# Block 0's expert outputs: rows of v gathered by token and summed over slots in four column groups of TensorE, in place of rows gathered by slot and summed token by token

## The chip, the cores and the metric

One core of one Trainium2 chip. The metric is the device time of one execution in microseconds (us). The kernel before was run three times.

## What is computed

One decoder layer over 512 tokens of width 1024: a mixer (matrix memory and differential attention), cross attention into 256 memory rows, and PEER, a channel mixer that picks 128 of 16384 experts for each token; then a final norm. Everything is float32. The change touches PEER alone, and of it the last line, for the first 128 tokens:

```python
def peer(h, w_pq, sub_keys, peer_u, peer_v):        # 4 blocks of 128 tokens
    def block(xb):
        q = (xb @ w_pq).reshape(PEER_BLOCK, PEER_HEADS, 2, PEER_HALF)
        sc = jnp.einsum('thcd,hcnd->thcn', q, sub_keys)
        ...                                          # top 16 of each half, top 16 of their sums
        u = peer_u[eidx]                             # eidx: 128 tokens x (8 heads x 16) experts
        act = jax.nn.gelu(jnp.einsum('td,thkd->thk', xb, u), approximate=False)
        coef = (gate * act).astype(xb.dtype)
        return jnp.einsum('thk,thkd->td', coef, peer_v[eidx])
```

With c[t, s] the coefficient of token t's slot s (128 slots), the sum is y[t] = sum over s of c[t, s] * v[eidx[t, s]], with 4 KB for each row of v.

## The kernel before

**Order of the work.** Block 0 (tokens 0 to 127) goes first through mixer, cross attention and key scores, then `route(0)` (top-k on DVE) gives its expert indices `eidx` and gates. Blocks 1 to 3 go together through the mixers (about 300 to 625 us) and then through `tail([2, 3, 1])`: cross attention (`cs`, `ct`, `co`, `cot`), query projection (`pqt`) and key scores (`rs`). Then come the routes of blocks 2 and 3 and of block 1. For blocks 2 and 3 the kernel builds a dense table W of gates over all experts, 64 tiles of 4 tokens each (L1052 to L1077: DVE compares, ACT scales and copies them to `oi` and `oj`, PE multiplies them into `wps`, ACT copies the product to W). From 1019 us to the end, 128 expert blocks are multiplied for blocks 2 and 3 in the dense stage. Blocks 0 and 1 take the sparse way, with gathered rows.

**The feeder.** Block 0's sparse work is woven into the work on blocks 1 to 3. `feed(where)` adds `PACE[where]` steps to what is owed at certain points of the program, and takes as many steps from a generator. The first generator, `sparse_dots(0)`, gathers u rows (one gather of 128 rows, 512 KB, for each slot) and takes dot products. The second, `sparse_sums(0)`, gathers the v rows of slot s for all 128 tokens (partition = token, L904, an indirect DMA that POOL issues into one of four buffers tagged `u`), and adds them:

- in the tail (slots 0 to 67) on DVE: `vacc = v * c + vacc`, L991 and L993;
- from the route stage on (slots 68 to 111) on PE: ACT scales an identity matrix by the slot's coefficients (`dg`, L985), and two matmuls with 128x128 weights `dg` and 128x512 of the rows add into PSUM (`vpe`, L987);
- slots 112 to 127 on DVE again.

A scheduler orders each engine's instructions when the program is built; at run time each engine works through its own list and waits where something is not ready. From the route stage on the gathers are kept in the program's order.

**PSUM.** The tail has three pools of banks (`ps` 3, `pa` 3, `pb` 2), the route and W stages two (`ps` 4, `pa` 4).

Names for what follows: a *slot* is one gather of the kernel before; a *tile* is one of W's 64 tiles; `trp` are the three transposes at the end of `route(2)` and `route(3)`.

Of the kernel before, what the change touches and what calls it, by code (L numbers as in the profile page):

```python
# [20 lines left out]
S = 512  # L21
D = 1024
# [8 lines left out]
SLOTS = HEADS * TOPK  # L31
# [3 lines left out]

U0A, U1A = (1,), ()

PACE = {"proj": 0.9, "ml": .8, "da": 1, "ca": 1.2, "route": 4, "W": .6, "half": 1.05}

LOW = ("pool",) * 8 + ('pool', 'dve', 'dve', 'dve', 'pool', 'dve', 'dve', 'dve')  # L40
LOW_FIRST = ('dve', 'dve', 'dve', 'dve', 'dve', 'dve', 'dve', 'dve')

PE_END = 111


def skewed(items, *stages, after=None):
# [39 lines left out]
def layer_kernel(ctx, tc, x, mem, norm_mix_g, w_in, conv_w, b_igate, b_fgate, ml_norm_g,  # L86
# [16 lines left out]
    keep = ctx.enter_context(tc.tile_pool(name="keep", bufs=1))  # L103
    dram = ctx.enter_context(tc.tile_pool(name="dram", bufs=1, space=DRAM))
    pctx = [ExitStack()]
    ctx.callback(lambda: pctx[0].close())

    def open_psum(name, **n):
        pctx[0].close()
        pool = pctx[0].enter_context(tc.tile_pool(name=name, bufs=1, space=PSUM))  # L110
        return [lambda nm, tag=tag, k=k: pool.tile([P, 512], F32, tag=tag, name=nm, bufs=k) for tag, k in n.items()]

    psums = open_psum("psumf", ps=3, pa=3, pb=2)

# [9 lines left out]
    ident = const.tile([P, P], F32, name="ident")  # L124
# [46 lines left out]
    def ft(shape, tag, name, bufs=2, dt=F32):  # L171
        return home[0].tile(shape, dt, tag=tag, name=name, bufs=bufs)
# [243 lines left out]
    feeder, owed = [], [0.0]  # L416
    in_step, on_pe, in_psum = [False], [False], [None]

    def feed(where, n=1):

        owed[0] += n * PACE[where]
        while owed[0] >= 1 and feeder:
            if next(feeder[0], None) is None:
                feeder.pop(0)
            else:
                owed[0] -= 1
# [16 lines left out]
        proj_tok(w_cv, 0, D, mT, 2, "mv", ev_v)  # L443
        nc.sync.dma_start(mv_d, mv)

    small, convs = [], [None]

    def queued_behind(ins, first):
        if first is not None:
            tc.add_manual_dep(ins.ins, first.ins.name,  # L450
                              mybir.DependencyInfo(mybir.DependencyClass.NoSync, mybir.DependencyReason.DATA))
# [359 lines left out]
    def route(T, scs, dense, tile_):  # L811

        gate = ft([P, SLOTS], "gate", f"gate{T}", bufs=1) if dense else keep.tile([P, SLOTS], F32, tag="gate", name=f"gate{T}", bufs=2)
        eidx = None if dense else keep.tile([P, SLOTS], I32, tag="eidx", name=f"eidx{T}", bufs=2)
        If = ft([P, SLOTS], "If", f"If{T}", bufs=1)
        Jf = ft([P, SLOTS], "Jf", f"Jf{T}", bufs=1)
        for q in range(2):
# [66 lines left out]
            nc.vector.reciprocal(gsum, gsum)  # L884
            nc.vector.tensor_tensor(gt, gt, gsum.unsqueeze(2).to_broadcast([P, 4, TOPK]), op=OP.mult)
            feed("route")
        if not dense:
            return eidx, gate
        tr = ft([P, 3, P], "tr", f"tr{T}")
        tp = ps(f"trp{T}")  # L890
        for i, t in enumerate((If, Jf, gate)):
            nc.tensor.transpose(tp[:, i * P:(i + 1) * P], t, ident)
        nc.scalar.copy(tr, tp[:, :3 * P].rearrange("p (a t) -> p a t", a=3))
        return tr

    def u_tile(name, shape=(P, D), dt=F32):
        return keep.tile(list(shape), dt, tag="u", name=name, bufs=4)


    to_gather, ahead = [], []  # L900

    def gather(src, eidx, s, name):
        u = u_tile(name)
        g = nc.gpsimd.indirect_dma_start(out=u, out_offset=None, in_=src,  # L904
                                         in_offset=bass.IndirectOffsetOnAxis(ap=eidx[:, s:s + 1], axis=0))
        if on_pe[0]:
            tc.keep_in_program_order(g)
# [12 lines left out]
    def finish(blocks, ys):  # L920

# [22 lines left out]
                nc.vector.scalar_tensor_tensor(x2[:, sl], x2[:, sl], r[:, 0:1], gf[:, sl], op0=OP.mult, op1=OP.mult)  # L944
                nc.sync.dma_start(outf[T * P:(T + 1) * P, sl], x2[:, sl])

    coefs, lane = {}, [None]

    def sparse_dots(T, eidx, gate, aside):

# [19 lines left out]
        nc.vector.tensor_mul(gate, act, gate)  # L970
        coefs[T] = gate

    def sparse_sums(T, eidx):

        act = coefs[T]
        acc = in_psum[0](f"vaccp{T}") if in_psum[0] else keep.tile([P, D], F32, tag="hv", name=f"vacc{T}", bufs=2)
        pe, last = None, None
        for s in range(SLOTS):
            v = gathered()
            c = act[:, s:s + 1]  # L980
            if on_pe[0] and 0 < s <= PE_END:
                if pe is None:
                    pe = [pa(f"vpe{T}{n}") for n in range(2)]
                dg = rp.tile([P, P], F32, tag="dg", name=f"dg{T}_{s}", bufs=2)
                nc.scalar.activation(dg, ident, AF.Copy, scale=c)  # L985
                for n in range(2):
                    nc.tensor.matmul(pe[n], lhsT=dg, rhs=v[:, n * 512:(n + 1) * 512],  # L987
                                     start=last is None, stop=s == PE_END)
                last = s
            elif s == 0:  # L990
                nc.vector.tensor_scalar(acc, v, c, None, op0=OP.mult)  # L991
            else:
                nc.vector.scalar_tensor_tensor(acc, v, c, acc, op0=OP.mult, op1=OP.add)  # L993
            if pe and s == PE_END:
                for n in range(2):
                    sl = slice(n * 512, (n + 1) * 512)
                    nc.vector.tensor_add(acc[:, sl], acc[:, sl], pe[n])
                pe = None
            lane[0] = pe
            yield s  # L1000
        finish([T], [acc])

# [14 lines left out]
    plan(0, r0[0])  # L1017
    feeder.append(sparse_dots(0, *r0, aside=U0A))
    feeder.append(sparse_sums(0, r0[0]))
    x1 = mixers(1, 3, hT1)  # L1020
    fctx.close()
    rp = rctx.enter_context(tc.tile_pool(name="routes", bufs=1, side="right", reuse_waits="tile"))
    home[0] = bctx.enter_context(tc.tile_pool(name="tail", bufs=1, reuse_waits="tile"))
    rings.update({"big": 2, "w": 8, "w4": 6})
    scs = {}
# [7 lines left out]
    def score(T, pq):  # L1033
        scs[T] = key_scores(T, pq, wide)

    order = [2, 3, 1]
    tail(order, [x1[T - 1] for T in order], True, w4, score)
    bctx.close()
    home[0] = rp
    psums[:] = open_psum("psumd", ps=4, pa=4)  # L1040
    on_pe[0] = True
    trs = [route(T, scs[T], True, scratch) for T in (2, 3)]
    r1 = route(1, scs[1], False, scratch)
# [6 lines left out]
    iota4 = op.tile([P, P, 4], BF16, name="iota4")  # L1050
    nc.gpsimd.tensor_copy(iota4, iota_n.unsqueeze(2).to_broadcast([P, P, 4]))
    for tt in range(NDENSE):  # L1052
        tr = trs[tt]
        ij = op.tile([P, 2, P], BF16, tag="ij", name=f"ij{tt}", bufs=1)
        nc.vector.tensor_copy(ij, tr[:, 0:2, :])
        for t4 in range(0, P, 4):
            eqs = []
            for a in range(2):
                e = op.tile([P, P, 4], BF16, tag=f"eq{a}", name=f"eq{tt}{t4}{a}", bufs=2)
                nc.vector.tensor_tensor(e, iota4, ij[:, a, t4:t4 + 4].unsqueeze(1).to_broadcast([P, P, 4]), op=OP.is_equal)  # L1060
                eqs.append(e)
            oi = op.tile([P, 4, P], F32, tag="oi", name=f"oi{tt}{t4}", bufs=3)
            oj = op.tile([P, 4, P], F32, tag="oj", name=f"oj{tt}{t4}", bufs=3)
            wps = ps(f"wps{tt}{t4}")
            nc.scalar.copy(oj, eqs[1].rearrange("p j q -> p q j"))
            for q in range(4):
                g = tr[:, 2, t4 + q:t4 + q + 1]
# [13 lines left out]
    owed[0] = 0.0  # L1081
    on_pe[0] = False
    rctx.close()
    pools = pctx[0].enter_context
    pctx[0].close()
    pq_ = pctx[0].enter_context(tc.tile_pool(name="psume", bufs=1, space=PSUM))
    in_psum[0] = lambda nm: pq_.tile([P, D], F32, tag="hv", name=nm, bufs=1)
    dp = ctx.enter_context(tc.tile_pool(name="dense", bufs=1, side="right", reuse_waits="tile"))
# [145 lines left out]
```

## Time and profile before

| what | us |
|---|---|
| runs of the kernel before | 1885.2, 1883.58, 1882.15 (median 1883.58) |
| the profiled execution's own time | 1875.28 |
| its span, first to last instruction | 1873.5 |
| busy: PE / DVE / POOL / ACT | 1591.3 / 1449.2 / 1062.8 / 806.9 |
| mean granted TensorE clock | 0.924 of full speed |

The span is the time from the first instruction to the last in one profiled execution; busy times are what each engine spent in instructions that the profiler recorded. "PEld" is TensorE's loading of weights, which overlaps the products. A float32 matmul leaves two records on PE, so counts of records are twice those of matmuls. A wait is the idle time of an engine before an instruction, with what ended it.

### The profile page before, as it was taken

To read this page: it belongs to the slowest core of one execution; us is meant where nothing else is said; L and a number is where in the kernel's file an instruction comes from. 1 tells how busy PE (TensorE), PEld (TensorE's weight loads), DVE (VectorE), ACT (ScalarE), POOL (GpSimd) and SP (SyncE) were. 2 spreads that over 40 slices of the span, in tenths; PEclk is the share of its full clock that TensorE was granted. 3 is DMA by queue.
4 is the path that set the end of the run, shared out by engine and by line. 5 is a ranking of instruction groups with operands and counts; after the bars stand their busy time and mean duration, and the time that the engine had idled before them with its cause. 6 is when DMAs were issued, how large, how long until landed. Compare 5 with 4: busy or idle time off the path is not lost.

```text
span 1873.5 us, 27679 instructions
## 1 busy us (share of the span) xinstructions
PE 1591.3 (85%) x9223; PEld 1330.1 (71%) x9223; DVE 1449.2 (77%) x3042; ACT 806.9 (43%) x1836; POOL 1062.8 (57%) x864
## 2 busy tenths in 40 slices
PE   7999796787647788899966999999999999999986
PEld 6798686685337467763655877777787778777765
DVE  4354498878878467999985888889888888888874
ACT  3553423535432122133999444444444444444433
POOL 2000136677766456345430877778787777777754
PEclk9899878898569899899988999999999999999998
DMA  7758615787777988677660999999999999999983
GB/s 240 236 185 272 217 50 175 231 294 262 234 237 248 369 289 295 203 217 257 191 229 32 323 339 336 331 331 335 326 339 333 331 330 334 337 333 322 335 303 118
DMA packets 211456, 501.15 MB, mean 267 GB/s; under 512 B 20793, under 2 KB 90481, under 8 KB 210545
## 3 DMA queue, kind: packets, MB, share of 16 engines
q0 software_dynamic: 74304, 270.57, 42.6%
q1 hardware_dynamic: 137008, 228.82, 36.0%
q8 instruction: 72, 1.18, 0.3%
q14 instruction: 72, 0.58, 0.1%
HBM read 490.93 MB, written 8.39 MB: 267 GB/s over the span
## 4 chain that ended last, share of the span: by engine, by line
DMA 26%; DVE 23%; PE 15%; issue 13%; ACT 11%; POOL 10%; SPq 1%; POOLq 0%; ACTq 0%; DVEq 0%
DMA vd<-in_peer_v_dram 13%; DMA v<-in_peer_v_dram,eidx 7%; DMA u<-in_peer_u_dram,eidx 5%; DVE uL L1129 4%; DVE u L966 4%; ACT vH L1137 4%; POOL vL L1138 4%; PE cqt_o L320 3%; POOL u L904 3%; ACT uH L1128 2%; DVE vacc L993 2%; PE vpe L987 2%; ACT oi L1069 2%; DVE ua L1156 1%; DVE vaccp L993 1%
## 5 line engine op out<-in xcount | busy, mean ns | idle before, releaser
L904 POOL DMA_INDIRECT u<-in_peer_u_dram,eidx x256 | 309.5, 1209 | 220.4 <-DVE u L966 104.9
L904 POOL DMA_INDIRECT v<-in_peer_v_dram,eidx x256 | 284.7, 1112 | 242.0 <-DVE vaccp L993 57.8
L1129 DVE TENSOR_TENSOR uL<-ud,uH 128x512 fp32r<-128x512 f32 x256 | 307.6, 1238 | 112.7 <-ACT uH L1128 110.2
L1138 POOL TENSOR_TENSOR vL<-vd,vH 128x512 fp32r<-128x512 f32 x256 | 352.8, 1395 | 57.4 <-ACT vH L1137 34.6
L312 PE MATMUL ua<-hH,uH 128*128 128x256 f32 x1024 | 290.4, 284 | 3.1 <-ACT hH L1101 3.1
L313 PE MATMUL ua<-hL,uH 128*128 128x256 f32 x1024 | 290.8, 284 | 0.2 <-DVE hL L1102 0.2
L314 PE MATMUL ua<-hH,uL 128*128 128x256 f32 x1024 | 290.6, 284 | 0.0
L313 PE MATMUL acc<-vL,pH 128*128 128x512 f32 x512 | 223.2, 436 | 53.6 <-POOL vL L1138 50.9
L1158 ACT CAST pH<-ua 128x256 fp32r<-128x256 f32 x128 | 47.7, 372 | 396.5 <-DVE ua L1156 396.5
L312 PE MATMUL acc<-vH,pH 128*128 128x512 f32 x512 | 203.3, 397 | 9.2 <-ACT vH L1137 9.2
L312 PEld LDWEIGHTS ua<-hH,uH 128*128 128x128 f32 x1024 | 196.8, 192 | 8.7 <-ACT hH L1101 3.3
L314 PE MATMUL acc<-vH,pL 128*128 128x512 f32 x512 | 202.7, 396 | 0.0
L966 DVE SCALAR_TENSOR_TENSOR u<-u,h3k 128x1024 f32<-128x1024 f32 x112 | 155.6, 1396 | 59.3 <-DMA u<-in_peer_u_dram,eidx 59.0
L313 PEld LDWEIGHTS ua<-hL,uH 128*128 128x128 f32 x1024 | 196.9, 192 | 5.8 <-DVE hL L1102 0.5
L314 PEld LDWEIGHTS ua<-hH,uL 128*128 128x128 f32 x1024 | 197.0, 192 | 0.0
L313 PEld LDWEIGHTS acc<-vL,pH 128*128 128x128 f32 x512 | 97.1, 190 | 131.0 <-POOL vL L1138 116.3
L1137 ACT CAST vH<-vd 128x512 fp32r<-128x512 f32 x256 | 154.9, 622 | 52.6 <-DMA vd<-in_peer_v_dram 48.7
L993 DVE SCALAR_TENSOR_TENSOR vaccp<-v,gate,vaccp 128x1024 f32<-128x1024 f32 x127 | 162.2, 1278 | 3.6 <-DMA v<-in_peer_v_dram,eidx 3.0
L966 DVE SCALAR_TENSOR_TENSOR u<-u,h3p 128x1024 f32<-128x1024 f32 x128 | 154.3, 1208 | 2.3 <-DMA u<-in_peer_u_dram,eidx 2.1
L1128 ACT CAST uH<-ud 128x512 fp32r<-128x512 f32 x256 | 145.7, 616 | 0.7 <-DVE hL L1102 0.7
L993 DVE SCALAR_TENSOR_TENSOR vacc<-v,gate,vacc 128x1024 f32<-128x1024 f32 x83 | 106.2, 1279 | 22.8 <-DMA v<-in_peer_v_dram,eidx 22.5
L312 PEld LDWEIGHTS acc<-vH,pH 128*128 128x128 f32 x512 | 97.6, 191 | 26.9 <-ACT vH L1137 9.8
(642 smaller groups left out, 3385.5 us busy)
## 6 DMA issues: line engine op xcount, KB each, us to landing
ud<-in_peer_ut_dram SPq DMA_DIRECT2D x128, 512.0 KB, 6.8
vd<-in_peer_v_dram SPq DMA_DIRECT2D x256, 256.0 KB, 4.7
qkg_w<-in_w_in_dram SPq DMA_DIRECT2D x16, 512.0 KB, 4.9
dag_w<-in_w_in_dram SPq DMA_DIRECT2D x16, 512.0 KB, 6.6
wog_w<-in_w_out_dram SPq DMA_DIRECT2D x16, 512.0 KB, 5.3
vg_w<-in_w_in_dram SPq DMA_DIRECT2D x8, 512.0 KB, 3.8
og_w<-in_w_in_dram SPq DMA_DIRECT2D x8, 512.0 KB, 5.7
dvg_w<-in_w_in_dram SPq DMA_DIRECT2D x8, 512.0 KB, 3.9
```

The source lines that it names most:

```text
L312: nc.tensor.matmul(o, lhsT=l[0], rhs=r[0], start=start, stop=False)
L313: nc.tensor.matmul(o, lhsT=l[0], rhs=r[1], start=False, stop=False)
L314: nc.tensor.matmul(o, lhsT=l[1], rhs=r[0], start=False, stop=stop)
L320: nc.tensor.matmul(o, lhsT=l, rhs=r, start=start, stop=stop)
L904: g = nc.gpsimd.indirect_dma_start(out=u, out_offset=None, in_=src, in_offset=bass.IndirectOffsetOnAxis(ap=eidx[:, s:s + 1], axis=0))
L966: nc.vector.scalar_tensor_tensor(u, u, 1.0, h3, op0=OP.mult, op1=OP.mult, accum_out=act[:, s:s + 1])
L993: nc.vector.scalar_tensor_tensor(acc, v, c, acc, op0=OP.mult, op1=OP.add)
L1128: nc.scalar.copy(H, r[:, sl])
L1129: nc.vector.tensor_sub(L, r[:, sl], H.bitcast(F32))
L1137: nc.scalar.copy(H, v)
L1138: nc.gpsimd.tensor_sub(L, v, H.bitcast(F32))
L1158: nc.scalar.copy(H, a)
```

## The change

The v rows of block 0 are gathered by token, not by slot: one gather brings the 128 rows of one token (partition = slot). For that, `route(0)` also transposes its index table (`eidxT`: two DVE operations, one PE transpose, one copy). `token_sums(0)` replaces `sparse_sums(0)`. It transposes the coefficients once (`cT`, slots on partitions), and takes the tokens four at a time: group g holds the tokens g, 32 + g, 64 + g and 96 + g. For each of 32 groups ACT copies four coefficient columns into a strip of zeros `zs` (two halves in turn), so that a window of 32 columns of `zs` is zero but for column g; then eight matmuls with 128x32 weights and 128x512 of gathered rows add into two PSUM banks, where token 32j + g has the rows 32j to 32j + 31 (column group j). Their order is fixed: j = 3, 2, 1, 0 for the first half of the row, then for the second. All 32 groups add into the same two banks, so there is no DVE sum, no `dg` and no `lane` any more; `finish` adds the banks to the residual.

The gathers use six buffers in turn, four of tag `u` and two of tag `hv`, and up to two are asked for ahead. The generator yields None, and takes nothing, until the two banks exist, which is when the tail begins. PSUM in the tail becomes `ps` 3, `pa` 2, `pb` 1 and the two banks; after it `ps` 6 and the two banks. Three paces change. The tile `tr` is split into `ij` (BF16, written by ACT) and `gt`, which removes a DVE cast for each of blocks 2 and 3.

```diff
-PACE = {"proj": 0.9, "ml": .8, "da": 1, "ca": 1.2, "route": 4, "W": .6, "half": 1.05}
+PACE = {"proj": 0.9, "ml": .8, "da": 1, "ca": 1.6, "route": 5, "W": .8, "half": 1.05}
...
         while owed[0] >= 1 and feeder:
-            if next(feeder[0], None) is None:
+            got = next(feeder[0], -1)
+            if got is None:
+                owed[0] = 0.0
+            elif got == -1:
                 feeder.pop(0)
...
+        if T == 0:
+            tp = ps(f"trp{T}")
+            nc.tensor.transpose(tp[:, :P], If, ident)
+            turned.append(keep.tile([P, P], I32, tag="eidx", name="eidxT", bufs=2))
+            nc.vector.tensor_copy(turned[0], tp[:, :P])
...
-    def gathered():
+    def gathered(more=0):
-        while to_gather and len(ahead) < (4 if in_step[0] else 1):
+        while to_gather and len(ahead) < (4 if in_step[0] else 1 + more):
...
+            to_gather.extend((vf, by_token, 32 * j + g, f"v{T}_{g}_{j}", (4 * g + j) % 6 > 3)
+                             for g in range(32) for j in range(4))
...
+    def token_sums(T):
+        while not vsum:
+            yield None
+        tp = ps(f"ctp{T}")
+        nc.tensor.transpose(tp[:, :P], coefs[T], ident)
+        cT = keep.tile([P, SLOTS], F32, tag="gate", name=f"cT{T}_", bufs=2).rearrange("p (j g) -> p j g", j=4)
+        nc.scalar.copy(cT, tp[:, :P].rearrange("p (j g) -> p j g", j=4))
+        acc = [vsum[0](f"vpe{T}{n}") for n in range(2)]
+        for g in range(32):
+            c0 = 32 * (g % 2)
+            nc.scalar.copy(zs[0][:, :, c0 + 31:c0 + 32], cT[:, :, g:g + 1])
+            rows_ = []
+            for j in range(4):
+                rows_.append(gathered(2))
+                if j < 3:
+                    yield g
+            mm = None
+            for n in range(2):
+                for j in (3, 2, 1, 0):
+                    m = nc.tensor.matmul(acc[n][32 * j:32 * j + 32, :], lhsT=zs[0][:, j, c0 + 31 - g:c0 + 63 - g],
+                                         rhs=rows_[j][:, n * 512:(n + 1) * 512], start=g == 0, stop=g == 31,
+                                         skip_group_check=True)
+                    queued_behind(m, mm)
+                    mm = m
+            yield g
+        finish([T], [acc])
...
-            if on_pe[0] and 0 < s <= PE_END:
-                if pe is None:
-                    pe = [pa(f"vpe{T}{n}") for n in range(2)]
-                dg = rp.tile([P, P], F32, tag="dg", name=f"dg{T}_{s}", bufs=2)
-                nc.scalar.activation(dg, ident, AF.Copy, scale=c)
-                for n in range(2):
-                    nc.tensor.matmul(pe[n], lhsT=dg, rhs=v[:, n * 512:(n + 1) * 512],
-                                     start=last is None, stop=s == PE_END)
...
+    psums[:] = open_psum("psumt", ps=3, pa=2, pb=1)
+    vpool = vctx.enter_context(tc.tile_pool(name="psumv", bufs=1, space=PSUM, side="right"))
+    vsum.append(lambda nm: vpool.tile([P, 512], F32, tag="vpe", name=nm, bufs=2))
     order = [2, 3, 1]
     tail(order, [x1[T - 1] for T in order], True, w4, score)
...
-    psums[:] = open_psum("psumd", ps=4, pa=4)
+    psums[:] = open_psum("psumd", ps=6)
```

Where the instructions now stand, at three places. First PE at the start of the W stage, in the kernel before: `vpe` rows are matmuls of a slot (two each), `wps` rows those of a tile (four each), `trp` the transposes of block 3's route.

```order
L987 MATMUL vpe_6444<-v_100_7395,dg_100_7397 128x512
L987 MATMUL vpe_6445<-v_100_7395,dg_100_7397 128x512
L892 MATMUL trp_6844<-ident,If_6597 128x128
L1073 MATMUL wps_7116<-oi_7114,oj_7115 128x128 x4
L1073 MATMUL wps_7139<-oi_7137,oj_7138 128x128 x2
L892 MATMUL trp_6844<-ident,Jf_6598 128x128
L892 MATMUL trp_6844<-ident,gate_6596 128x128
L1073 MATMUL wps_7139<-oi_7137,oj_7138 128x128 x2
L1073 MATMUL wps_7156<-oi_7154,oj_7155 128x128 x4
L987 MATMUL vpe_6444<-v_101_7435,dg_101_7437 128x512
```

In the kernel before the first tile stands behind slot 100: 33 slots (68 to 100) lie between the tail's last product and W's first, and 11 more among the first tiles; 49 of the 64 tiles follow the last of them with nothing of the sums between.

The same engine in the changed kernel, a little further on (v_20_3 are the rows of group 20, column group 3):

```order
L1010 MATMUL vpe_5308<-v_20_3_7021,zs 32x512
L1010 MATMUL vpe_5308<-v_20_2_6908,zs 32x512
L1010 MATMUL vpe_5308<-v_20_1_6897,zs 32x512
L1010 MATMUL vpe_5308<-v_20_0_6895,zs 32x512
L1106 MATMUL wps_7217<-oi_7215,oj_7216 128x128 x2
L1106 MATMUL wps_7237<-oi_7235,oj_7236 128x128 x4
L1106 MATMUL wps_7256<-oi_7254,oj_7255 128x128 x4
L1106 MATMUL wps_7275<-oi_7273,oj_7274 128x128 x3
L1010 MATMUL vpe_5307<-v_21_3_7038,zs 32x512
L1010 MATMUL vpe_5307<-v_21_2_7036,zs 32x512
```

Groups 0 to 15 now stand in the tail, 16 to 19 between the tail and W's first tile, and 20 to 31 among the tiles, some 12 `wps` matmuls (three tiles) apart; 110 `wps` matmuls (27.5 tiles) follow group 31.

POOL's list of gathers in the changed kernel, in the route stage:

```order
L915 DMA v_18_2_6776<-in_peer_v_dram,eidxT 128x1024
L915 DMA v_18_3_6778<-in_peer_v_dram,eidxT 128x1024
L915 DMA v_19_0_6780<-in_peer_v_dram,eidxT 128x1024
L915 DMA v_19_1_6782<-in_peer_v_dram,eidxT 128x1024
L915 DMA v_19_2_6891<-in_peer_v_dram,eidxT 128x1024
L915 DMA v_19_3_6893<-in_peer_v_dram,eidxT 128x1024
L915 DMA v_20_0_6895<-in_peer_v_dram,eidxT 128x1024
L915 DMA v_20_1_6897<-in_peer_v_dram,eidxT 128x1024
```

With six buffers in turn, v_19_2 and v_19_3 take the buffers of v_18_0 and v_18_1, and v_20_0 and v_20_1 those of v_18_2 and v_18_3. Before, each slot's gather took the buffer of the fourth slot before it.

## Rows read from the trace of the kernel before

**Rows 1.** Stretches: PE, PEld, DVE, ACT and POOL busy (records), granted clock, DMA, GB/s.

```profile
628.00:822.00 194.00, 173.35 (x994) 143.43 (x993) 143.55 (x375) 44.03 (x111) 86.77 (x77) 0.95 0.81 273
...
720.00:755.00 35.00, 26.52 (x190) 24.44 (x190) 23.00 (x32) 9.44 (x28) 19.92 (x16) 0.90 0.89 301
755.00:790.00 35.00, 29.66 (x172) 26.41 (x171) 35.00 (x154) 6.24 (x12) 10.82 (x11) 0.90 0.59 186
...
856.00:890.00 34.00, 30.53 (x68) 11.65 (x67) 33.56 (x199) 9.95 (x19) 17.52 (x17) 1.00 0.78 252
...
985.00:1018.00 33.00, 21.65 (x136) 18.47 (x134) 17.05 (x47) 33.00 (x87) 0.00 (x0) 0.95 0.00 0
```

**Rows 2.** The chain that ended last, from 620 us: start, us, what.

```profile
628.49 41.92 PE cqt_o L320 x128
...
881.21 8.98 PE vpe L987 x20
...
890.31 1.34 PE wps L1073 x12
...
893.21 3.44 PE vpe L987 x8
```

**Rows 3.** The same chain, where W ends and the dense stage begins.

```profile
1016.57 0.91 ACT oi L1069 x3
1017.47 0.54 ACT oj L1065
...
1018.06 1.17 PE wps L1073 x8
...
1019.74 0.63 ACT hH L1101
```

**Rows 4.** PE's waits between 628 and 822 us: total, times, longest.

```profile
PE ct L748 <- DVE cp L742: 10.2, 3, 5.6
PE fT1p L361 <- DVE h L774: 5.3, 1, 5.3
PE pqt_o L320 <- DMA pqt_w<-in_w_pq_dram: 2.9, 2, 2.7
PE cot_o L320 <- ACT oT L204: 1.3, 1, 1.3
```

**Rows 5.** Groups of instructions, shapes apart.

```profile
L993 DVE SCALAR_TENSOR_TENSOR vacc<-v,gate,vacc 128x1024 f32<-128x1024 f32 x83 | 106.2, 1279 | 22.8 <-DMA v<-in_peer_v_dram,eidx 22.5
L985 ACT ACTIVATE dg<-ident,gate 128x128 f32<-128x128 f32 x44 | 17.4, 400 | 44.8 <-PE vpe L987 44.5 <-DVE gate L970 0.4
```

**Rows 6.** PE's timeline in the tail, products over 64 rows among full ones.

```profile
800.42 1.61 PE L803 MATMUL rs<-skT,pq 64*128 64x128 f32 x20
...
802.60 0.48 PE L803 MATMUL rs<-skT,pq 64*128 64x128 f32 x2
803.01 1.60 PE L320 MATMUL pqt_o<-fT,pqt_w 128*128 128x128 f32 x12
804.55 1.16 PE L803 MATMUL rs<-skT,pq 64*128 64x128 f32 x8
805.63 6.63 PE L320 MATMUL pqt_o<-fT,pqt_w 128*128 128x128 f32 x57
```

**Rows 7.** POOL's timeline: gathers after an idle time.

```profile
866.24 0.94 POOL L904 DMA_INDIRECT v<-in_peer_v_dram,eidx  x1 [3.57 <-PE vpe L987]
867.48 0.93 POOL L904 DMA_INDIRECT v<-in_peer_v_dram,eidx  x1 [0.30 <-issue]
868.72 0.94 POOL L904 DMA_INDIRECT v<-in_peer_v_dram,eidx  x1 [0.30 <-issue]
869.96 0.94 POOL L904 DMA_INDIRECT v<-in_peer_v_dram,eidx  x1 [0.30 <-PE vpe L987]
```

**Rows 8.** DMA issues: us to landing, from 866.2, 867.4, 868.7, and 822 to 890.

```profile
v<-in_peer_v_dram,eidx POOLq DMA_INDIRECT x1, 4.5
...
v<-in_peer_v_dram,eidx POOLq DMA_INDIRECT x1, 5.3
...
v<-in_peer_v_dram,eidx POOLq DMA_INDIRECT x1, 6.0
...
v<-in_peer_v_dram,eidx POOLq DMA_INDIRECT x33, 5.3
```

More of the change, by code (lines that the diff above doesn't have):

```diff
@@ L36 @@
 U0A, U1A = (1,), ()
-PACE = {"proj": 0.9, "ml": .8, "da": 1, "ca": 1.2, "route": 4, "W": .6, "half": 1.05}
+PACE = {"proj": 0.9, "ml": .8, "da": 1, "ca": 1.6, "route": 5, "W": .8, "half": 1.05}
 LOW = ("pool",) * 8 + ('pool', 'dve', 'dve', 'dve', 'pool', 'dve', 'dve', 'dve')
 LOW_FIRST = ('dve', 'dve', 'dve', 'dve', 'dve', 'dve', 'dve', 'dve')
-PE_END = 111
 def skewed(items, *stages, after=None):
@@ L106, in layer_kernel @@
     ctx.callback(lambda: pctx[0].close())
+    vctx = ExitStack()
     def open_psum(name, **n):
@@ L444, in mem_front @@
         nc.sync.dma_start(mv_d, mv)
-    small, convs = [], [None]
+    small, convs, turned = [], [None], []
     def queued_behind(ins, first):
@@ L878, in route @@
                 nc.vector.scalar_tensor_tensor(eidx[:, sl], If[:, sl], float(P), Jf[:, sl], op0=OP.mult, op1=OP.add)
+                if T == 0:
+                    nc.vector.scalar_tensor_tensor(If[:, sl], If[:, sl], float(P), Jf[:, sl], op0=OP.mult, op1=OP.add)
             gt = gate[:, sl].rearrange("p (h k) -> p h k", h=4)
@@ L886, in route @@
             feed("route")
+        if T == 0:
+            tp = ps(f"trp{T}")
+            nc.tensor.transpose(tp[:, :P], If, ident)
+            turned.append(keep.tile([P, P], I32, tag="eidx", name="eidxT", bufs=2))
+            nc.vector.tensor_copy(turned[0], tp[:, :P])
         if not dense:
             return eidx, gate
-        tr = ft([P, 3, P], "tr", f"tr{T}")
+        ij, gt = ft([P, 2, P], "trij", f"trij{T}", dt=BF16), ft([P, P], "trg", f"trg{T}")
         tp = ps(f"trp{T}")
@@ L892, in route @@
             nc.tensor.transpose(tp[:, i * P:(i + 1) * P], t, ident)
-        nc.scalar.copy(tr, tp[:, :3 * P].rearrange("p (a t) -> p a t", a=3))
-        return tr
+        nc.scalar.copy(ij, tp[:, :2 * P].rearrange("p (a t) -> p a t", a=2))
+        nc.scalar.copy(gt, tp[:, 2 * P:3 * P])
+        return ij, gt
     def u_tile(name, shape=(P, D), dt=F32):
@@ L900, in layer_kernel, with gather @@
     to_gather, ahead = [], []
-    def gather(src, eidx, s, name):
-        u = u_tile(name)
+    def gather(src, eidx, s, name, in_hv=False):
+        u = keep.tile([P, D], F32, tag="hv", name=name, bufs=2) if in_hv else u_tile(name)
         g = nc.gpsimd.indirect_dma_start(out=u, out_offset=None, in_=src,
@@ L908, in gather, with plan @@
         return u
-    def gathered():
-        while to_gather and len(ahead) < (4 if in_step[0] else 1):
+    def gathered(more=0):
+        while to_gather and len(ahead) < (4 if in_step[0] else 1 + more):
             ahead.append(gather(*to_gather.pop(0)))
         return ahead.pop(0)
-    def plan(T, eidx):
-        for src, c in ((uf, "u"), (vf, "v")):
-            to_gather.extend((src, eidx, s, f"{c}{T}_{s}") for s in range(SLOTS))
+    def plan(T, eidx, by_token=None):
+        to_gather.extend((uf, eidx, s, f"u{T}_{s}") for s in range(SLOTS))
+        if by_token is None:
+            to_gather.extend((vf, eidx, s, f"v{T}_{s}") for s in range(SLOTS))
+        else:
+            to_gather.extend((vf, by_token, 32 * j + g, f"v{T}_{g}_{j}", (4 * g + j) % 6 > 3)
+                             for g in range(32) for j in range(4))
     def finish(blocks, ys):
@@ L945, in finish @@
                 nc.sync.dma_start(outf[T * P:(T + 1) * P, sl], x2[:, sl])
-    coefs, lane = {}, [None]
+    coefs, vsum = {}, []
     def sparse_dots(T, eidx, gate, aside):
@@ L976, in sparse_sums @@
         acc = in_psum[0](f"vaccp{T}") if in_psum[0] else keep.tile([P, D], F32, tag="hv", name=f"vacc{T}", bufs=2)
-        pe, last = None, None
         for s in range(SLOTS):
@@ L980, in sparse_sums @@
             c = act[:, s:s + 1]
-            if on_pe[0] and 0 < s <= PE_END:
-                if pe is None:
-                    pe = [pa(f"vpe{T}{n}") for n in range(2)]
-                dg = rp.tile([P, P], F32, tag="dg", name=f"dg{T}_{s}", bufs=2)
-                nc.scalar.activation(dg, ident, AF.Copy, scale=c)
-                for n in range(2):
-                    nc.tensor.matmul(pe[n], lhsT=dg, rhs=v[:, n * 512:(n + 1) * 512],
-                                     start=last is None, stop=s == PE_END)
-                last = s
-            elif s == 0:
+            if s == 0:
                 nc.vector.tensor_scalar(acc, v, c, None, op0=OP.mult)
@@ L993, in sparse_sums @@
                 nc.vector.scalar_tensor_tensor(acc, v, c, acc, op0=OP.mult, op1=OP.add)
[L994 to L999, printed above, removed]
             yield s
@@ L1016, in layer_kernel @@
     r0 = route(0, key_scores(0, pqs[0], w4), False, w4)
-    plan(0, r0[0])
+    plan(0, r0[0], turned[0])
     feeder.append(sparse_dots(0, *r0, aside=U0A))
-    feeder.append(sparse_sums(0, r0[0]))
+    feeder.append(token_sums(0))
     x1 = mixers(1, 3, hT1)
@@ L1022, in layer_kernel @@
     rp = rctx.enter_context(tc.tile_pool(name="routes", bufs=1, side="right", reuse_waits="tile"))
+    zs = [rp.tile([P, 4, 95], F32, name="zs")]
+    nc.gpsimd.memset(zs[0], 0.0)
     home[0] = bctx.enter_context(tc.tile_pool(name="tail", bufs=1, reuse_waits="tile"))
@@ L1052, in layer_kernel @@
     for tt in range(NDENSE):
-        tr = trs[tt]
-        ij = op.tile([P, 2, P], BF16, tag="ij", name=f"ij{tt}", bufs=1)
-        nc.vector.tensor_copy(ij, tr[:, 0:2, :])
+        ij, gt = trs[tt]
         for t4 in range(0, P, 4):
@@ L1066, in layer_kernel @@
             for q in range(4):
-                g = tr[:, 2, t4 + q:t4 + q + 1]
+                g = gt[:, t4 + q:t4 + q + 1]
                 if q < 3:
@@ L1083, in layer_kernel @@
     rctx.close()
-    pools = pctx[0].enter_context
     pctx[0].close()
+    vctx.close()
     pq_ = pctx[0].enter_context(tc.tile_pool(name="psume", bufs=1, space=PSUM))
```

## The prediction

> **What bounds the kernel now.** I read the chain that ended last first, then stretches of the part from 628 to 1020 us, then waits, groups and timelines inside it. From 1019.7 us the dense stage takes over [rows 3], and no instruction of it is changed, so the change is worth what it moves this start. Before it lie three stretches. In the tail (628.5 to 822.2) PE is busy 173.4 of 194 us [rows 1], beginning with one projection of 41.9 us [rows 2]; the rest are waits, the longest for DVE, which has the sums in its queue: 10.2 us for `cp`, 5.3 for `h` [rows 4]. In the route stage PE works on the slots, 30.5 of 34 us [rows 1], and W's first tile stands behind them in PE's list: it begins when slot 100 is done, at 890.3 [rows 2]. In W the last 33 us show ACT busy throughout with 136 PE records of eight a tile [rows 1]: 17 tiles, 1.94 us each. 64 tiles from 890.3 to 1018.1 make 2.0 each, so ACT paces W nearly from its start.
>
> **A group's products.** The 128x512 pass of today takes 3.44 / 8 = 0.43 us a record [rows 2], two records a matmul. Eight matmuls are 16 records: 6.88 us if they run singly, 3.44 if two at a time, 1.72 if all four column groups run together. No row of before has column groups. The nearest are products over 64 rows, which leave half the array free: 20 records in 1.61 us, 0.08 each, against 0.117 for 57 full ones in 6.63 [rows 6], some of the 20 without a partner. So parts of the array do work side by side, and I take four at a time; 1.72 and 6.88 stay as bounds. By the Trainium skill ("TensorE: Matmul & The Clock Gate", Part 3: Packing small matmuls) three column tiles gave 2.38 times the speed, nearly what the rows here make likely; at that share of the ideal a group would take an estimated 2.2 us, and the sum would be some 14 us larger.
>
> Going into and out of the other shape costs something: two row-group records begin at 802.60 and the full product behind them at 803.01, where a pair takes about 0.11; eight begin at 804.55 and are followed at 805.63, where four pairs take 0.45 [rows 6]. That is 0.3 to 0.6 us; since PE mostly waits ahead of a group anyway, I add 0.23 and take 1.95 us a group. The Trainium skill ("TensorEngine Tiling (Array Packing)", Key Properties) states that a change of tiling mode drains TensorE, a rule against this change; the rows agree as far as they go, and the full 0.6 on each group would add about 12 us.
>
> **A group's gathers.** The two last gathers of a group reuse the buffers of the first two of the group before, which come free only when that group's last products are done. So the gathers no longer trickle, one buffer at a time; each group is followed by a wait: POOL starts 0.30 us after PE's release, the second gather 1.24 later [rows 7], and it lands 4.5 to 5.3 after its issue [rows 8]. I take 4.9, so 0.3 + 1.24 + 4.9 = 6.4 us, and with the products 8.35 us for four tokens where nothing longer stands between. Bounds: 1.72 + 0.3 + 1.24 + 4.5 = 7.8, and 6.0 for the landing [rows 8] gives 9.5. Today four slots take 4 x 68/33 = 8.2 us (33 slots between 822.2 and 890.3).
>
> **The sum.**
> - *Tail, 16 groups.* 173.4 + 16 x 1.95 = 204.6 us of PE. The DVE sums go (83 of 1.28 us, most of them here) [rows 5], and the waits on `cp` and `h` with most of them. 7 us are left for waits: on weights and `oT` 4.2 [rows 4], and a few pieces between groups shorter than 6.4 us (eight `pqt` matmuls and eight transposes make some 3.5, at two records of 0.11 us each). `pb` 1 and `pa` 2 delay a product by its evacuation at times; that is in the 7. The tail ends at 628.5 + 211.6 = 840, 18 late.
> - *Route, groups 16 to 19.* 4 x 8.35 = 33 us, 3 for transposes and a lower clock: W begins at 876, 14 early. DVE, 33.6 of 34 us busy before [rows 1], is freed of the tail's sums and runs ahead, so block 3's route is ready.
> - *W.* Groups 20 to 31 stand three tiles apart in PE's list. Three tiles take ACT 5.9 us, and the ring 8.35: PE stands still at the group, the finished `oi` and `oj` fill up, and ACT waits. From 874 twelve periods are 100 us: 974. The 27.5 tiles behind them take 53.4, the last product 1.2 [rows 3]: W ends at 1029, against 1018.
> - *At nothing.* 44 `dg` of 0.40 us go from ACT [rows 5], 32 small copies come; ACT waits in W anyway. `eidxT` adds four short instructions to `route(0)`, far ahead of the first v gather. The first dense loads on SP are now behind the gathers (their `hv` buffers), 974 at the latest and 50 us ahead of need. `finish(0)` lies beside the 27 tiles. The cast of `ij` goes from a DVE that is not late.
>
> In all +11 us: 1886.3 against the profiled execution's own 1875.3. That execution stands 8.3 us below the median of the three runs, so on the scale of the median **1894.6**. About 0.2% (3.8 us) is what a measurement can tell from no change.
>
> **Rivals.**
> *Faster: the groups fall into PE's idle time.* They take up all the waits in the tail (173.4 + 31.2, end at 833), and PE, no longer idle for `cp`, keeps its clock: 0.90 was granted from 720 to 790 [rows 1], and full speed over these 70 us gives 5 back: 828. With the lower ring, 7.8, W begins at 862, and its end is 859 + 94 + 55 = 1008, 10 early: about 1874. For it: the waits in rows 4 are DVE's. Against: short pieces behind a 6.4 us ring. It decides where tail end plus 16 rings comes below 960 (today's 1018, less 55 for the last tiles and 3 around the transposes): with the tail at 840 a ring of 7.5, with 828 one of 8.2.
> *Two at a time.* If only neighbours overlap, as rows 6 show pairs alone, a group takes 3.44 + 0.23: 1.7 more on 32 groups, 55 us; 11 + 55 gives about 1950.
> *No overlap.* The column groups run one by one and the change does not do what it says: 6.88 + 0.23, 5.2 more on each, 165 us: about 2060. Against it stands the first line of rows 6.
>
> **How the numbers follow.** Forecast (four at a time, ring visible in W) 0.55, from 1880 to 1910 by the bounds; of it 0.12 within 3.8 us of the median before, 0.03 faster and 0.40 slower. Faster rival 0.30. Two at a time 0.11, none 0.04. So faster 0.33, same 0.12, slower 0.55. The range goes from 1868 (the faster rival with 6 us more) to 1925 (a ring of 9.5 in the 16 groups after the tail adds 18, the shape changes 12); the 15 in 100 of the last two rivals lie above it.
>
> **What would show it.** Right: `vpe` products of some 1.7 to 2 us for 16 records; the tail's last `rs` near 840 us; PE waiting on v rows ahead of groups 16 to 31, 5 us and more where three tiles lie between; ACT with idle time in W until about 974 and none afterwards; the last `wps` near 1029. Wrong: groups of 3.4 us or longer; ACT busy through W (ring hidden); the tail ending by 830; the dense stage itself taking another time.

## The result, and the profile after

The changed kernel takes 1910.99 us (median; 1909.41 to 1912.59), the kernel before, run beside it, 1883.88 us: a ratio of 1.0144, interval 1.0127 to 1.0162. It is slower, as forecast, but by 27 us and not by 11; the time lies inside the range (1868 to 1925), the size of the move is wrong. In a later session the same pair gave 1913.2 and 1874.28, a ratio of 1.0214 (1.0178 to 1.0249): the change stays near 1912, the kernel before varies from session to session. The profiled execution of the change (1910.83 us) spans 1908.7 us, 35 more than the one of before. Counted from the tail's first product to the dense stage's first, so without what happens ahead of the tail, the kernel before takes 393.8 and 394.9 us in its two profiles, the change 442.4 and 443.1: 48 us more, where the forecast had 11.

The stretches of the changed kernel, tail, route stage, W with groups, W without (columns as in [rows 1]):

```profile
617.40:841.80 224.40, 204.10 (x1249) 146.27 (x1249) 94.71 (x480) 49.65 (x130) 68.81 (x73) 0.96 0.64 218
842.00:882.30 40.30, 15.36 (x67) 3.07 (x67) 34.71 (x204) 8.16 (x21) 15.39 (x16) 0.50 0.62 207
882.30:1005.80 123.50, 77.64 (x492) 44.14 (x488) 56.57 (x218) 77.22 (x197) 49.34 (x48) 0.83 0.62 204
1005.80:1057.00 51.20, 36.06 (x224) 31.29 (x220) 29.45 (x78) 50.48 (x130) 4.02 (x5) 0.97 0.31 109
```

The tail ends at 841.8, forecast 840, but it began at 617.4 and lasted 224 us, forecast 211.6. The route stage runs with PE busy 15 of 40 us and a granted clock of 0.50, the lower level (1.2 GHz). In W with groups ACT is busy 77 of 123 us, and only afterwards, 50.5 of 51, does it set the pace. W ends at 1056.6 and not at 1029.

PE's timeline of the same kernel, with the groups (`vpe`) and what stands between them:

```profile
655.74 1.92 PE L1010 MATMUL vpe<-v,zs 128*32 128x512 f32 x16
657.60 4.78 PE L320 MATMUL cqt_o<-cTt__5245,cqt_w 128*128 128x384 f32 x14
...
784.63 1.94 PE L361 MATMUL fT1p<-ident,h 128*128 128x128 f32 x8 [6.56 <-DVE h L777]
787.52 3.62 PE L1010 MATMUL vpe<-v,zs 128*32 128x512 f32 x16 [0.95 <-DMA v<-in_peer_v_dram,eidxT]
...
857.79 3.64 PE L1010 MATMUL vpe<-v,zs 128*32 128x512 f32 x16 [7.53 <-DMA v<-in_peer_v_dram,eidxT]
868.19 3.65 PE L1010 MATMUL vpe<-v,zs 128*32 128x512 f32 x16 [6.75 <-DMA v<-in_peer_v_dram,eidxT]
...
962.05 3.40 PE L1010 MATMUL vpe<-v,zs 128*32 128x512 f32 x16 [3.86 <-DMA v<-in_peer_v_dram,eidxT]
965.38 2.94 PE L1106 MATMUL wps<-oi,oj 128*128 128x128 f32 x24
972.24 3.42 PE L1010 MATMUL vpe<-v,zs 128*32 128x512 f32 x16 [3.91 <-DMA v<-in_peer_v_dram,eidxT]
...
1003.92 1.92 PE L1010 MATMUL vpe<-v,zs 128*32 128x512 f32 x16 [2.72 <-DMA v<-in_peer_v_dram,eidxT]
1005.77 3.58 PE L1106 MATMUL wps<-oi,oj 128*128 128x128 f32 x28
```

In the tail a group's 16 records take 1.86 us up to the next product (655.74 to 657.60). That is 3.7 times as fast as 16 single records of 0.43 us [rows 2]: all four column groups do run together. Behind a wait of 6.7 to 7.5 us the same 16 records take 3.64 at a granted clock of 0.50 (857.6 to 861.5; 1.00 from 655.7 to 657.6), and in W 3.25 to 3.64 for ten of the twelve groups, 1.92 for the other two. From 857.79 to 868.19 a period is 10.4 us, forecast 8.35: 3.64 of products and 6.76 of ring. About three tiles stand in a W period (24 `wps` records in the one from 962.05 to 972.24, 10.2 us long; 18 to 28 in the others).

POOL's timeline beside it shows the ring:

```profile
861.72 0.95 POOL L915 DMA_INDIRECT v<-in_peer_v_dram,eidxT  x1 [6.07 <-PE vpe L1010]
862.98 0.95 POOL L915 DMA_INDIRECT v<-in_peer_v_dram,eidxT  x1 [0.30 <-issue]
...
872.06 0.95 POOL L915 DMA_INDIRECT v<-in_peer_v_dram,eidxT  x1 [4.85 <-PE vpe L1010]
```

The group at 857.79 ends at 861.43; 0.29 us later its successor's two missing gathers start, 1.26 apart, and the second is used 5.21 after its start (868.19). Before, most gathers of the route stage were issued one at a time, 1.7 to 2.7 us apart, as their buffers came free.

The chain that ended last runs through this ring as long as groups stand in W; here it is from 956.87 on:

```profile
956.87 5.14 DMA v<-in_peer_v_dram,eidxT
...
962.05 3.40 PE vpe L1010 x16
965.45 1.33 PE wps L1106 x10
...
966.97 5.23 DMA v<-in_peer_v_dram,eidxT
```

PE's waits, in the tail (617 to 842, the first two lines) and behind it (842 to 1058):

```profile
PE vpe L1010 <- DMA v<-in_peer_v_dram,eidxT: 12.5, 10, 2.9
PE fT1p L361 <- DVE h L777: 6.6, 1, 6.6
...
PE vpe L1010 <- DMA v<-in_peer_v_dram,eidxT: 68.5, 16, 7.5
PE wps L1106 <- ACT oi L1102: 16.3, 25, 1.7
```

Of [rows 4] the wait for `cp` is gone; the one for `h` is still there, longer than before, and 12.5 us of waits for gathered rows are new in the tail, 68.5 behind it.

### The profile page after: what moved, and what is told of

It reads as the page before. It is cut to its first block, busy times and chain, and to the rows that moved or that the text cites. A ratio compares the mean times of both kernels' runs of the same rounds, so it can differ in the third digit from the quotient of the medians.

```text
span 1908.7 us, 28083 instructions
## 1 busy us (share of the span) xinstructions
PE 1581.5 (83%) x9561; PEld 1299.0 (68%) x9561; DVE 1341.4 (70%) x2958; ACT 798.0 (42%) x1827; POOL 1039.7 (54%) x865
## 4 chain that ended last, share of the span: by engine, by line
DMA 15%; issue 12%; POOL 10%; ACT 7%; DVE 7%; PE 6%; POOLq 3%; ACTq 0%; DVEq 0%; SPq 0%
DMA vd<-in_peer_v_dram 8%; POOL vL L1171 6%; DMA v<-in_peer_v_dram,eidxT 5%; DVE uL L1162 3%; POOL v L915 3%; PE vpe L1010 3%; ACT vH L1170 3%; POOLq L1171 2%; DVE u L981 2%; POOL u L915 1%; ACT uH L1161 1%; ACT oi L1102 1%; DMA v<-in_peer_v_dram,eidx 1%; DVE vaccp L1028 1%; DVE ua L1189 1%
## 5 line engine op out<-in xcount | busy, mean ns | idle before, releaser
L915 POOL DMA_INDIRECT u<-in_peer_u_dram,eidx x256 | 313.9, 1226 | 216.7 <-DVE u L981 91.2
L915 POOL DMA_INDIRECT v<-in_peer_v_dram,eidxT x128 | 131.0, 1024 | 252.3 <-PE vpe L1010 216.5
L981 DVE SCALAR_TENSOR_TENSOR u<-u,h3k 128x1024 f32<-128x1024 f32 x112 | 150.9, 1354 | 52.1 <-DMA u<-in_peer_u_dram,eidx 51.6
L915 POOL DMA_INDIRECT v<-in_peer_v_dram,eidx x128 | 137.8, 1076 | 72.5 <-DVE vaccp L1028 52.5
L1010 PE MATMUL vpe<-v,zs 128*32 128x512 f32 x512 | 87.1, 813 | 81.0 <-DMA v<-in_peer_v_dram,eidxT 81.0
```

Source lines behind the costliest of these rows:

```text
L981: nc.vector.scalar_tensor_tensor(u, u, 1.0, h3, op0=OP.mult, op1=OP.mult, accum_out=act[:, s:s + 1])
L1010: m = nc.tensor.matmul(acc[n][32 * j:32 * j + 32, :], lhsT=zs[0][:, j, c0 + 31 - g:c0 + 63 - g], rhs=rows_[j][:, n * 512:(n + 1) * 512], s ...
```

## The experiments

Theory: behind the tail each group costs a ring (the gathers that can start only when the group before has freed its buffers), and its products run at the lower clock, since PE has just waited; and PE's standing order (three tiles to a period, 27.5 behind the last group) makes W pay for it. Rivals: the paces; transfers or DVE bound these stages whatever the order.

**The kernel before, again (e1_before_again).** No edit.

> The kernel before once more, for a second profile. The changed kernel's profile starts its tail 9 us earlier than the profile of before (619.7 against 628.5), and the profiled execution of before was 8 us below its own median, so that the profiles stand 35 us apart and the medians 27. If the early start belongs to the change, this profile starts the tail at 628 again, within 2 us. If it is what one execution differs from the next, the tail begins elsewhere (620 to 640) and the span is nearer 1882.

Measured: 1867.29 us (one run), span 1864.3. PE's tail begins at 620.0 (and the changed kernel's at 617.4, not at the 619.7 written above):

```profile
620.03 41.61 PE L320 MATMUL cqt_o<-cTt__5273,cqt_w 128*128 128x384 f32 x128
```

So executions of one kernel differ by 8 us in the place of the tail's start (620.0 and 628.5 for the kernel before; 613.0 to 623.9 in the eleven profiles of the changed kernel and its variants). The start fits the second outcome that I had written, the span neither. Stages are therefore compared by their lengths below, not by their places.

But not all of it is chance. From `route(0)`'s first key scores (`rs`, at 230 to 236 us) to block 0's first dot product it is 73.9 and 73.1 us in the two profiles of before, and 66.1 to 66.5 in all eleven others; from that dot product to the tail 314.7 to 322.3 in all thirteen. POOL's lists differ there, first before, then the change:

```profile
294.62 4.20 POOL L328 TENSOR_TENSOR vg_w0L<-vg_w,vg_w0H 128x1024 fp32r<-128x1024 f32 x1 [7.62 <-ACT vg_w0H L344]
299.01 2.62 POOL L904 DMA_INDIRECT u<-in_peer_u_dram,eidx  x1 [0.19 <-DVE ztg L525]
...
291.70 1.24 POOL L915 DMA_INDIRECT u<-in_peer_u_dram,eidx  x1 [13.28 <-DVE abf L862]
```

Before, the first gather of u rows stands behind a preparation of weights (`vg_w0L`); in the change that stands earlier in POOL's list (276.04), so some 7 us of the earlier start belong to the change.

**The old paces (e2_paces_back).**

```diff
-PACE = {... "ca": 1.6, "route": 5, "W": .8, ...}
+PACE = {... "ca": 1.2, "route": 4, "W": .6, ...}
```

> The change with the three paces of before (ca 1.2, route 4, W .6). Theory (each group behind the tail costs a period of about 10.4 us, 6.8 of waiting for gathers and 3.6 of products at half clock, and holds W's tiles up): two groups move from the tail to the stages behind it, so the tail is some 4 us shorter and the rest up to 20 longer: 1905 to 1930. Rival (the paces made it slower): back towards 1884.

Measured: 1912.02 us beside 1875.49, ratio 1.0202 (1.0169 to 1.0235). The paces are not the cause.

**Sixteen groups evenly over W (e3_even).** `last_w` is the last `wps` matmul written so far; the edit holds a group's first product behind it on PE.

```diff
-PACE = {... "ca": 1.6, "route": 5, "W": .8, ...}
+PACE = {... "ca": 1.6, "route": 0, "W": 1.0, ...}
...
-            mm = None
+            mm = last_w[0]
```

> No groups in the route stage (pace 0), and the 16 left ones spread evenly over W, each held behind the fourth tile after the one before it. Theory: PE and ACT make four tiles (7.8 us) inside one group's period (10.4 us), nothing is left to do behind the last group: W ends at 842 + 16 x 10.4 = 1009 in place of 1057, and the time is about 1864, below the kernel before. Rival (W is not held up by the groups, but the transfers or PE's clock bound both): no change, 1900 to 1915.

Measured: 1903.66 us beside 1875.49, ratio 1.0168 (1.0128 to 1.0209): a miss by 40 us, and inside the rival's range. PE's timeline shows why:

```profile
874.49 0.47 PE L902 MATMUL trp<-ident,If 128*128 128x128 f32 x1 [32.22 <-DVE If L879]
...
1037.95 3.64 PE L1010 MATMUL vpe<-v,zs 128*32 128x512 f32 x16 [6.54 <-DMA v<-in_peer_v_dram,eidxT]
1052.85 0.58 PE L312 MATMUL ua<-hH,uH 128*128 128x256 f32 x1 [11.25 <-ACT uH L1161]
```

PE waits 32 us for block 3's top-k on DVE. In the change groups stand there, so that part of the route stage was paid for anyway; here these 32 us went by without a group, and the last group ended at 1041.6. From its first tile W lasts 167 us, as long as the theory's 16 periods of 10.4, but it starts 32 later than the theory had it. A W bound by its gathers is what the rival says too, so this run does not decide between them; e8, with a better place for the groups, does.

**Pairs of products (e4_pairs).** Behind the tail only:

```diff
+                if on_pe[0] and j == 1:
+                    products(g, c0, rows_, (1, 0))
...
+            products(g, c0, rows_, (3, 2) if done[0] == g else (3, 2, 1, 0))
```

> Behind the tail a group's products are issued in two pairs, columns 1 and 0 as soon as their two rows are there, then 3 and 2, so that buffers come free two at a time and four gathers are under way while a pair is multiplied; only two column groups can overlap. Theory (the wait comes of freeing all buffers at once): four tokens take about 8 us in place of 10.4, 16 groups 38 us less: about 1873. Rival (the period is the products' and the clock's): two pairs at half clock are 7.2 us and the period stays near 10.4: 1905 to 1915.

Measured: 1860.97 us beside 1875.49, ratio 0.9938 (0.9915 to 0.9961): 52 us below the change at 1913, and below the kernel before. PE's timeline, then stretches (the route stage, W with pairs, W without):

```profile
846.63 1.91 PE L1004 MATMUL vpe<-v,zs 128*32 128x512 f32 x8 [1.55 <-DMA v<-in_peer_v_dram,eidxT]
849.54 1.91 PE L1004 MATMUL vpe<-v,zs 128*32 128x512 f32 x8 [1.00 <-DMA v<-in_peer_v_dram,eidxT]
852.20 1.91 PE L1004 MATMUL vpe<-v,zs 128*32 128x512 f32 x8 [0.75 <-DMA v<-in_peer_v_dram,eidxT]
```

```profile
841.00:872.70 31.70, 20.75 (x78) 4.52 (x77) 28.71 (x160) 8.35 (x23) 19.07 (x21) 0.89 0.90 314
872.70:948.00 75.30, 74.17 (x436) 38.60 (x436) 55.99 (x244) 68.00 (x172) 44.25 (x42) 1.00 0.87 305
948.00:1007.00 59.00, 41.04 (x258) 35.08 (x256) 34.63 (x91) 59.00 (x153) 4.05 (x5) 1.00 0.26 94
```

A pair takes 1.91 us, two of them 3.8: as long for PE as a whole group at the lower clock. Yet four tokens now take 6.9 us (30 pairs from 843.17 to 946.14), since gathers run while a pair is multiplied: 305 GB/s where the change moved 204. With the shorter waits PE keeps full clock in W (1.00), and ACT is busy 68 of 75 us. As PE spends the same time on products as at the lower clock, what this run saved is the waiting; how pairs would fare at the lower clock is not shown.

**Filling the waits (e5_filled).**

```diff
+WARM = 16
...
+            if on_pe[0]:
+                wm = psums[1](f"warm{g}")
+                for _ in range(WARM):
+                    m = nc.tensor.matmul(wm[:, :P], lhsT=ident, rhs=ident, start=True, stop=True)
+                    queued_behind(m, mm)
+                    mm = m
...
-    psums[:] = open_psum("psumd", ps=6)
+    psums[:] = open_psum("psumd", ps=5, warm=1)
```

> The change, with 16 products of the identity by itself (128x128, 0.22 us each at full clock, 3.5 us in all) behind each group from the route stage on, into a PSUM bank that nobody reads. They do nothing but fill PE's wait for the next group's rows (6.8 us in the route stage, about 4 in W). Theory (the half clock that PE is granted after each wait doubles the group's products, 3.6 in place of 1.9 us): the groups take about 1.9 us, a period is 8.7 in place of 10.4, 16 groups 27 us less: 1884 to 1890 where the change takes 1911. Rival (the ring alone sets the period): no change, or some us more for the added products.

Measured: 1901.99 us beside 1880.71, ratio 1.0130 (1.0062 to 1.0197). PE's timeline:

```profile
845.85 1.92 PE L1011 MATMUL vpe<-v,zs 128*32 128x512 f32 x16 [1.37 <-DMA v<-in_peer_v_dram,eidxT]
847.71 3.84 PE L1019 MATMUL warm<-ident 128*128 128x128 f32 x32
854.57 1.92 PE L1011 MATMUL vpe<-v,zs 128*32 128x512 f32 x16 [3.03 <-DMA v<-in_peer_v_dram,eidxT]
...
863.44 3.60 PE L1011 MATMUL vpe<-v,zs 128*32 128x512 f32 x16 [3.18 <-DMA v<-in_peer_v_dram,eidxT]
```

Where the filling kept the clock, the group is 1.92 us and the period 8.7 (845.85 to 854.57), as the theory has it. It did so only in part: of the five groups ahead of W's first tile two took 1.92 us and three 3.39 to 3.60 (granted clock 0.53 from 863.4 to 867.0). Later in W the scheduler wove the added products between the tiles, with periods of some 12 us, so the gain is 9 to 11 us and not 27. The clock's price for one group is shown; what all the groups together would gain is not.

**Column by column (e6_by_column).**

```diff
-            for n in range(2):
-                for j in (3, 2, 1, 0):
+            for j in (3, 2, 1, 0):
+                for n in range(2):
```

> The same products in another fixed order: column group by column group, both halves of the row in turn, so that two products in a row use the same 32 columns. Theory (products overlap only with neighbours in other columns): a group takes 4.3 us in the tail in place of 1.9, 16 groups in the tail 38 us more, and the rest 16 times up to 2.4 us at full clock (more at half): 1950 to 2000. Rival (each column group works through its own products whatever the order): 1.9 us a group and no change, 1905 to 1915.

Measured: 1914.98 us beside 1880.71, ratio 1.0185 (1.0110 to 1.0260). The theory falls, the rival holds; a group of the tail:

```profile
679.83 1.95 PE L1010 MATMUL vpe<-v,zs 128*32 128x512 f32 x16 [0.97 <-DMA v<-in_peer_v_dram,eidxT]
```

1.95 us, as for most groups of that tail, with two products in a row on the same columns. The fixed order is worth nothing measurable here.

**No groups in the tail (e7_no_tail).** The sums get their two banks only behind the tail (`vsum.append` moved below it).

> The sums begin only behind the tail, so all 32 groups stand in the route and W stages (the tail holds none). This tells what 16 groups cost the tail. Theory (their PE time, 31 us, is added to a tail that PE bounds): the tail's last rs product comes some 30 us earlier than in the change, about 811 us, and the whole is slower, since 32 periods of 10.4 us follow: 811 + 333 = 1144 for W's end, about 2000. Rival (the tail is longer for its fewer PSUM buffers or a later start): the tail still ends near 840.

Measured: 1987.18 us (one run). The tail lasts from 623.9 to 795.5, 171.6 us, with PE busy 166.9 at a granted clock of 1.00. PE's wait for `h` in it:

```profile
PE fT1p L361 <- DVE h L777: 1.7, 1, 1.7
```

Against 224.4 us in the change, 16 groups cost the tail 53 us, and not the 31 of the theory. PE is busy 37 longer (204.1 against 166.9): 30 of products (16 x 1.86), the rest with the granted clock at 0.96 in place of 1.00. It waits 16 longer, 12.5 of that for rows and 5 for `h`. The tail of before, with its DVE sums, is 193.7 us long, 22 more than this one, which has no sums.

**Even, behind a filled route stage (e8_even_after_route).** As e3, with three groups in the route stage and five tiles between the others:

```diff
-PACE = {... "ca": 1.6, "route": 5, "W": .8, ...}
+PACE = {... "ca": 1.6, "route": 2.7, "W": .81, ...}
```

> Three groups in the route stage, where PE has to wait for DVE's top-k of block 3 until 874 us in any case, and the other 13 spread evenly over W, each held behind the fifth tile after the one before. Theory (in the change W's tiles are held up three to a period, and 27 tiles are left behind the last group): five tiles take ACT 9.7 us and hide in a period of 10.4, W ends at 874 + 13 x 10.4 = 1009 in place of 1057, 45 us less: about 1866. Rival (even W is bound by the gathers and the clock, as e3_even ended no better than the change): 1895 to 1910.

Measured: 1866.93 us beside 1880.71, ratio 0.9934 (0.9904 to 0.9963). PE's timeline, then the stretch of W:

```profile
866.54 3.64 PE L1010 MATMUL vpe<-v,zs 128*32 128x512 f32 x16 [6.70 <-DMA v<-in_peer_v_dram,eidxT]
872.56 0.33 PE L902 MATMUL trp<-ident,If 128*128 128x128 f32 x1 [2.38 <-DVE If L879]
...
1001.88 1.16 PE L1106 MATMUL wps<-oi,oj 128*128 128x128 f32 x8
1011.63 0.58 PE L312 MATMUL ua<-hH,uH 128*128 128x256 f32 x1 [8.59 <-ACT hH L1134]
```

```profile
872.00:1003.00 131.00, 105.62 (x723) 75.84 (x723) 91.44 (x339) 125.92 (x325) 52.80 (x52) 0.92 0.64 209
```

W ends at 1003, 54 us ahead of the change, with the same groups, buffers and whole-group products: ACT is busy 126 of 131 us. Ten of the 54 are its earlier start (872.6, with one group fewer ahead of it, against 882.3). With five tiles to a period the ring costs W little: 131 us, where 64 tiles take ACT 124 at the rate of the prediction's lines. The clock went with it: ten of the thirteen groups in W take 1.92 or 1.93 us.

**Both, and both with block 1's top-k deferred (e9_pairs_even, e11_pairs_even_defer).** e9 joins the edits of e4 and e8. e11 adds, on DVE, `queued_behind` from the last operation of block 3's route to the first ones of block 1's, and sets route 1.2, W .92.

> The two edits that gained, together: pairs of products behind the tail (e4) and the remaining ones held evenly among W's tiles (e8). Theory (the ring of gathers and the tiles left behind the last group are two prices of one thing, the standing order of PE): W starts where block 3's top-k ends on DVE, about 873, and is bound by ACT alone, 64 x 1.93 = 124 us: it ends at 997 to 1000, against 1003 (e8) and 1007 (e4); 3 to 9 us below those, ratio to the kernel before 0.989 to 0.993. Rival (each gain needs the other's place): no better than e4 and e8, 0.993 to 0.996.

> As e9, and block 1's top-k is held behind block 3's on DVE (the two were mixed, and W's first tile waits for block 3's), with fewer pairs ahead of W. Theory (W's start is bound by DVE): block 3's indices are ready some 12 to 15 us earlier, W starts near 858 and ends at 982 to 988, 12 us below e9: ratio to the kernel before 0.982 to 0.987. Rival (W is then bound by the gathers, 16 x 6.9 us from 842 on, and by block 1's top-k on DVE among the tiles): W ends at 995 or later and nothing is gained on e9.

Measured: e9 1866.45 us beside 1874.28, ratio 0.9963 (0.9943 to 0.9983); e11 1872.03, ratio 0.9978 (0.9963 to 0.9993). Both theories missed; the rivals came closer. e9 ends its tiles early and then waits, and e11's top-k of block 3 was not earlier; from PE's timelines, first e9, then e11:

```profile
866.59 0.47 PE L902 MATMUL trp<-ident,If 128*128 128x128 f32 x1 [13.16 <-DVE If L879]
...
994.06 1.16 PE L1113 MATMUL wps<-oi,oj 128*128 128x128 f32 x8
...
1004.93 0.58 PE L312 MATMUL ua<-hH,uH 128*128 128x256 f32 x1 [9.71 <-ACT hH L1141]
```

```profile
879.86 0.47 PE L906 MATMUL trp<-ident,If 128*128 128x128 f32 x1 [25.73 <-DVE If L881]
```

The two gains do not add up: either edit brings W near the rate of ACT, and with the last group at W's very end the dense stage waits 9.7 us (e9), 13.2 (e11) or 8.6 (e8), against 3.1 in the change. In e8 its first loads (`h3d`) stand on SP behind another (`h3s`) that waits for the last group's products; they are issued from 1002.9 on, when W is done. In the change they are issued at 1012.4, 47 us ahead of need. The deferral gained nothing: from the tail's end to block 3's indices it is 31.8 us in e11 and 31.9 in e9; why, was not followed.

**The change again (e10_change_again).**

> The changed kernel once more, beside the same runs of the kernel before as the others: a ratio of 1.013 to 1.020, and a second profile, in which PE's groups behind the tail again take 3.3 to 3.65 us after their waits, and the tail again lasts 222 to 226 us from its first cqt product to its last rs product.

Measured: 1913.2 us beside 1874.28, ratio 1.0214 (1.0178 to 1.0249). Tail 615.7 to 838.7, 223 us, as expected; 13 of the 16 groups that follow it take 3.29 to 3.64 us, the other three 1.92 to 2.83. The ratio lies just above the range that I had given.

## Why the prediction was right in its direction and wrong in its size

- *A group's products, 1.95 us*: right in the tail (1.86), all four columns at once; "two at a time" and "no overlap" are out. From the three column tiles of the Trainium skill ("TensorE: Matmul & The Clock Gate", Part 3: Packing small matmuls) the prediction had estimated 2.2 us; the rows show less.
- *The step that failed: "with the products 8.35 us for four tokens", and "3 for transposes and a lower clock".* I had written down the ring behind each group, but carried a group's duration from a busy PE into stages where PE had just waited. There the granted clock is 0.50 (route) and 0.83 (W), and most groups take 3.25 to 3.65 us. A period of the route stage measured 10.4 in place of 8.35: 1.69 of products at the lower clock, 0.36 of a later landing. From the tail's end to the end of group 31 the sixteen periods took 164 us, forecast 134; the sixteen groups themselves took 52.7 in place of 31.2, so 21.5 of these 30 us are products at the lower clock, and the rest was not split further. The tiles behind group 31 took 51, forecast 55. With a tail that ended 2 late, W ended at 1057 and not at 1029.
- *The tail, "7 us are left for waits"*: a second term mis-sized. PE was busy 204.1 us, forecast 204.6, but it waited 20.3: the wait for `h` did not go with DVE's sums (6.6), and gathers cost 12.5. So the tail was 224 us long and not 212.
- *Luck:* the longer tail did not show in its end (841.8, forecast 840), only because that execution began its tail 11 us earlier than the profile I had read. Some 7 of the 11 are the change's own, by POOL's order in `route(0)` (e1), where the prediction counted four short instructions at nothing; the rest is what executions differ by. It made the miss in the time smaller than the 37 us between the tail's start and the dense stage.
- *W, held up by the groups*: right, and this is why the direction came out. e8 ends W 54 us earlier by other places for the groups, e4 50 by smaller batches. Both also raised the granted clock in W (0.92 and 1.00, against 0.83), so neither parts the order, the ring and the clock from each other, and the two gains do not add up.
- *"That execution stands 8.3 us below the median"*: the kernel before differs by more than that between executions and sessions (1862 to 1888), so the scale of the sum was uncertain by some 10 us in itself: +27 beside one set of runs, +39 beside another, +35 between the profiles. The sum also set W's end with its last product (1029) against one without it (1018 for 1019.2), 1.2 us too much.
- *The faster rival* did not come: the tail ended at 842 and not at 828, since groups and waits made it longer, and a ring with its products was 10.4 us and not 7.8. Its full clock held nearly in the tail (0.96), not in the stages whose length it needed.

## What to carry to other kernels

A duration read where an engine is busy does not hold where it will have to wait first: take TensorE's at the granted clock that the changed stretch will have. Operands that are consumed as one batch free their buffers as one batch, and with few buffers the next transfers then start only behind the products; consume them in smaller parts, even at a worse rate of products, or place enough work that is waiting for another engine inside the period. Where a scheduler fixes an engine's order, count what stands between two waits and what is left behind the last.

## What was not expected of the hardware

Column groups do not need their products to alternate: 16 records took 1.95 us with two products in a row on the same 32 columns (e6), as with alternating ones (1.92). And coming out of the column form costs little: the next product starts 1.86 us after a group of 16 records, 0.14 over the ideal 1.72, where the row-group rows had suggested 0.3 to 0.6 [rows 6].
